# A two-layer encoder in fp32 pairs: the hidden tiles of its feed-forward part in lots of 2, 6, 6, 4 and 4, and weight splits tied to a place in their engines' rows

## The chip, the cores and the metric

The kernel runs on one core of a Trainium2 chip. The metric is device time in microseconds (us), smaller is better. Engines are called by their names in the profile: PE is TensorE (PEld its weight loads), DVE is VectorE, ACT is ScalarE, POOL is GpSimd, SP is SyncE, which here only issues transfers. Each engine works its own row of instructions in order.

## The reference

Two layers over 512 tokens of width 1024, all in fp32. With the mixer A (a window of +-128 tokens) in layer 0 and the mixer B (all tokens) in layer 1:

```
x += rms_norm(w_o [12 token heads | 4 memory heads](rms_norm(x)))
x += rms_norm(SwiGLU(rms_norm(x)))        # silu(h Wg) * (h Wu), then @ Wd
```

The hidden width of SwiGLU is 2816, which is 22 tiles of 128.

## The kernel before, in words

**Pairs.** TensorE works on fp32r. Each fp32 operand is split into a hi part (a copy on ScalarE, L318) and a lo part (a subtraction on VectorE, L322), and each product is three matmuls: hi by hi, hi by lo, lo by hi (L308 to L310 for plain products).

**Lots.** The feed-forward part works the hidden tiles in lots: `LOTS = ((0, 2), (2, 8), (8, 14), (14, 22))`. For each hidden tile from the third on, gate and up come from seven block products (`seven`, L1131 to L1133, 256 columns, 84 matmuls a tile) in the manner of Strassen. When the last block of a tile is done, ScalarE takes Silu (L1184), VectorE multiplies by up (L1185), and `keep_hidden` splits the hidden tile into its pair: hi on ScalarE (L1007), lo on VectorE (L1008). With its first or second half of the lot's tiles, the sums and differences that the seven down products need are formed too (`low`, `high`, L1020 to L1031).

**Down.** The lots in `SEVEN` (the second and third, six tiles each) get their part of the down product as seven block products too (`down` calls `times`, L1257 to L1259, 512 columns): A11, A12, S2, S1, S3, S4, A22 in this order. Each result is added to the layer's output `o` in SBUF (`out_of`, L1267). A11's last steps and A12 follow the last tile's last block at once, so those of the steps that take older tiles stand first (`BY_UNIT`), and the last tile's come at the thirteenth matmul. The weights' block sums are made by transfers that add (`load_block`, the queue of POOL); `pairs` splits them. The last lot's down product is plain (`ffn_out`): for each row block of 128 tokens and each half of 512 columns three matmuls a tile, then `join` adds to `o` (L928), forms the mean square on ScalarE (L346), multiplies by the gain (L932); `post_norm` adds the residual (L814) and, in layer 0, writes the next layer's normed rows `h` (L822), which TensorE turns and VectorE and ScalarE split (`hrows`). In layer 1 the last row block is worked in two quarters (`ending`, L946, L950).

**Spares.** During the down products of layer 0's lots of six, `spare_load` fetches weights wq and wo of layer 1, and `spare_pair` splits them in halves (`c<-raw` on ScalarE, `s<-raw,c` on VectorE) and stores the pairs in DRAM; layer 1 then loads pairs. What is left of these units is split by `ahead` during the last lot's plain down product.

**Order.** TensorE's order is written out by hand. The rows of ScalarE, VectorE, POOL and SP are laid by a scheduler, which goes by its own estimates; `queue` and `issue_after` tie an instruction behind another. The pool of split weights holds four pairs, that of raw weights three.

## Time and profile before

| | |
|---|---|
| median of three runs | 1089.26 us (1089.0 to 1090.06) |
| profiled execution | 1091.68 us, its span 1089.9 us |
| TensorE busy | 1063.6 us (98%), 7364 matmuls |
| VectorE busy | 894.2 us (82%) |
| ScalarE busy | 693.5 us (64%) |
| granted clock of TensorE, mean | 0.994 |

Times in the rows of the trace count from the start of the span. A row of the timeline has the start, the duration, engine, line, operation, output and inputs, and in brackets how long the engine was idle before it and what released it. Rows of windows have the stretch, its length, the busy time of PE, PEld, DVE, ACT and POOL with their counts, then TensorE's granted clock, the share of the transfer engines and GB/s. Matmul durations overlap; what counts is the distance from start to start.

### The profile page before, as it was taken

To read this page: it belongs to the slowest core of one execution; us is meant where nothing else is said; L and a number is where in the kernel's file an instruction comes from. 1 tells how busy PE (TensorE), PEld (TensorE's weight loads), DVE (VectorE), ACT (ScalarE), POOL (GpSimd) and SP (SyncE) were. 2 spreads that over 40 slices of the span, in tenths; PEclk is the share of its full clock that TensorE was granted. 3 is DMA by queue.
4 is the path that set the end of the run, shared out by engine and by line. 5 is a ranking of instruction groups with operands and counts; after the bars stand their busy time and mean duration, and the time that the engine had idled before them with its cause. 6 is when DMAs were issued, how large, how long until landed. Compare 5 with 4: busy or idle time off the path is not lost.

```text
span 1089.9 us, 19990 instructions
## 1 busy us (share of the span) xinstructions
PE 1063.6 (98%) x7364; PEld 973.2 (89%) x7364; DVE 894.2 (82%) x1561; ACT 693.5 (64%) x1429; POOL 255.3 (23%) x405
## 2 busy tenths in 40 slices
PE   9999999999999989999999999999999999999997
PEld 7899887999879979998898888778999899899986
DVE  7889875978899979995887998767979888899954
ACT  7679884766646645663566888766766466556631
POOL 5673331211131100000443553313011111100001
PEclk9999999999999999999999999999999999999999
DMA  9721106456987894329752220136369769833243
GB/s 326 265 67 39 33 20 258 148 134 173 264 272 181 233 273 166 110 67 317 242 193 98 78 78 1 47 119 227 104 149 261 219 162 255 220 113 105 68 162 116
DMA packets 56978, 173.42 MB, mean 159 GB/s; under 512 B 6576, under 2 KB 6960, under 8 KB 56752
## 3 DMA queue, kind: packets, MB, share of 16 engines
q1 hardware_dynamic: 47376, 150.76, 40.4%
q0 software_dynamic: 9216, 20.98, 11.4%
q8 instruction: 58, 0.95, 0.4%
q10 hardware_dynamic: 288, 0.40, 0.1%
q14 instruction: 40, 0.33, 0.1%
HBM read 149.04 MB, written 16.78 MB: 152 GB/s over the span
## 4 chain that ended last, share of the span: by engine, by line
PE 82%; DVE 7%; ACT 4%; DMA 3%; issue 2%; POOL 2%; SPq 0%; DVEq 0%; POOLq 0%; ACTq 0%
PE ps L1131 11%; PE ps L1132 11%; PE ps L1133 11%; PE ps L309 9%; PE ps L308 9%; PE ps L310 9%; PE ps L1259 3%; PE ps L1257 3%; PE ps L1258 3%; PE tp L673 3%; PE o L687 2%; PE o L688 2%; PE s L612 1%; DMA raw<-in_wq_dram 1%; PE s L613 1%
## 5 line engine op out<-in xcount | busy, mean ns | idle before, releaser
L318 ACT ACTIVATE whi<-raw 128x512 fp32r<-128x512 f32 (+3 forms) x180 | 141.2, 804 | 93.6 <-issue 26.0
L322 DVE TENSOR_TENSOR wlo<-raw,whi 128x512 fp32r<-128x512 f32 (+3 forms) x176 | 157.8, 912 | 38.3 <-ACT whi L318 37.8
L1131 PE MATMUL ps<-hrows,whi 128*128 128x256 f32 x640 | 176.3, 275 | 0.1
L1132 PE MATMUL ps<-hrows,wlo 128*128 128x256 f32 x640 | 176.2, 275 | 0.0
L1133 PE MATMUL ps<-hrows,whi 128*128 128x256 f32 x640 | 176.2, 275 | 0.0
L308 PE MATMUL ps<-whi,hrows 128*128 128x256 f32 (+2 forms) x432 | 144.1, 333 | 0.0
L309 PE MATMUL ps<-wlo,hrows 128*128 128x256 f32 (+2 forms) x432 | 138.0, 319 | 1.6 <-DVE wlo L322 1.5
L310 PE MATMUL ps<-whi,hrows 128*128 128x256 f32 (+2 forms) x432 | 138.0, 320 | 0.0
L1132 PE MATMUL ps<-a,wlo 128*128 128x256 f32 x480 | 132.1, 275 | 0.0
L1131 PE MATMUL ps<-a,whi 128*128 128x256 f32 x480 | 132.1, 275 | 0.0
L1133 PE MATMUL ps<-a,whi 128*128 128x256 f32 x480 | 132.1, 275 | 0.0
L1131 PEld LDWEIGHTS ps<-hrows,whi 128*128 128x128 f32 x640 | 120.1, 188 | 0.8 <-ACT p L1137 0.3
L1132 PEld LDWEIGHTS ps<-hrows,wlo 128*128 128x128 f32 x640 | 120.1, 188 | 0.5
L1133 PEld LDWEIGHTS ps<-hrows,whi 128*128 128x128 f32 x640 | 120.1, 188 | 0.0
L663 POOL TENSOR_SCALAR p<-p,rd 128x256 f32<-128x256 f32 (+2 forms) x128 | 78.1, 628 | 102.8 <-DVE rd L660 66.2
L1132 PEld LDWEIGHTS ps<-a,wlo 128*128 128x128 f32 x480 | 90.1, 188 | 0.2
L1131 PEld LDWEIGHTS ps<-a,whi 128*128 128x128 f32 x480 | 90.1, 188 | 0.2
L1133 PEld LDWEIGHTS ps<-a,whi 128*128 128x128 f32 x480 | 90.1, 188 | 0.0
L309 PEld LDWEIGHTS ps<-wlo,hrows 128*128 128x128 f32 x432 | 81.6, 189 | 7.4 <-DVE wlo L322 2.5
L310 PEld LDWEIGHTS ps<-whi,hrows 128*128 128x128 f32 x432 | 81.3, 188 | 5.6 <-DVE hrows L336 0.3
L308 PEld LDWEIGHTS ps<-whi,hrows 128*128 128x128 f32 x432 | 81.4, 188 | 5.0
L318 ACT ACTIVATE whi<-rb 128x1024 fp32r<-128x1024 f32 x56 | 59.6, 1064 | 29.9 <-PE ps L1259 20.7
(231 smaller groups left out, 2854.0 us busy)
## 6 DMA issues: line engine op xcount, KB each, us to landing
raw<-in_wgu_dram SPq DMA_DIRECT2D x48, 512.0 KB, 4.6
rb<-in_wgu_dram SPq DMA_DIRECT2D x40, 512.0 KB, 3.9
raw<-in_wd_dram SPq DMA_DIRECT2D x18, 512.0 KB, 4.3
raw<-in_wq_dram SPq DMA_DIRECT2D x16, 512.0 KB, 5.3
raw<-in_wo_dram SPq DMA_DIRECT2D x16, 512.0 KB, 3.6
rb<-in_ws_dram SPq DMA_DIRECT2D x16, 512.0 KB, 7.6
rs<-in_ws_dram SPq DMA_DIRECT2D x28, 256.0 KB, 6.5
xt<-x SPq DMA_DIRECT2D x12, 512.0 KB, 4.9
```

The costliest lines, as they stand in the source:

```text
L308: mm(out, lh, rh, start=first, stop=False)
L309: mm(out, lh, rl, start=False, stop=False)
L310: mm(out, ll, rh, start=False, stop=last)
L318: a = nc.scalar.activation(hi, src, AF.Copy)
L322: b = nc.vector.tensor_sub(lo, src, hi.bitcast(F32))
L663: self.pooled = nc.gpsimd.tensor_scalar(hd["p"][z][:, :n], hd["p"][z][:, :n], rd[:, z:z + 1], 1.0, op0=OP.mult, op1=OP.mult)
L673: nc.tensor.transpose(tp[:, z], hd["p"][i][:, jj * P:(jj + 1) * P], self.ident)
L1131: mm(out, wh[:, s], rh, start=start and k == 0, stop=False, skip_group_check=True)
L1132: mm(out, wl[:, s], rh, start=False, stop=False, skip_group_check=True)
L1133: mm(out, wh[:, s], rl, start=False, stop=k == 3, skip_group_check=True)
L1257: mm(ps[t], lh, rh, start=fresh and i == 0, stop=False, skip_group_check=True)
L1258: mm(ps[t], lh, rl, start=False, stop=False, skip_group_check=True)
```

## The change

The last lot of eight tiles becomes two lots of four, and the first of these gets its down product as seven block products, with two tiles to a half. `SEVEN` now says how many tiles a half has. The block arrays of the weights become one per lot (`ws1` to `ws3`), a half of two tiles needs no third unit (`rs`), and A11 is cut into 2 + 2 steps where a half of three has 4 + 2 (`fill`). The spare splits: `spare_pair` stands one product later, behind the split of that product's weights, and each of its splits is tied behind the last weight split on ScalarE and on VectorE (`ends["pair"]`). `spare_load` does nothing in the lot of four, so that of two units which `ahead` worked in layer 0 only one is left, and layer 1 splits one wo unit itself.

```
-LOTS = ((0, 2), (2, 8), (8, 14), (14, 22))
-SEVEN, HALF = (1, 2), 3
+LOTS = ((0, 2), (2, 8), (8, 14), (14, 18), (18, 22))
+SEVEN = {1: 3, 2: 3, 3: 2}
...
                 hi, lo = [self.whl.tile([P, 1024], F32R, tag=z, name=f"w{z}", bufs=4) for z in ("hi", "lo")]
-                self.split(hi[:, :n], lo[:, :n], x)
+                ends["pair"] = self.split(hi[:, :n], lo[:, :n], x)
...
-        BY_ROW = [(i, t) for t in range(2) for i in range(HALF)]
-        BY_UNIT = [(0, 0), (1, 0), (0, 1), (1, 1), (2, 0), (2, 1)]
+        def by_row(h):
+            return [(i, t) for t in range(2) for i in range(SEVEN[h["lot"]])]
+
+        def by_unit(h):
+            return [(0, 0), (1, 0), (0, 1), (1, 1), (2, 0), (2, 1)][:2 * SEVEN[h["lot"]]]
+
+        def fill(h, z):
+            n = 2 * SEVEN[h["lot"]] - 2
+            return by_unit(h)[n:] if z else by_unit(h)[:n]
...
-        def spare_load():
-            if self.todo:
+        def spare_load(h):
+            if self.todo and SEVEN[h["lot"]] > 2:
...
                     hi, lo = temp("c"), temp("s")
-                    self.split(hi.bitcast(F32R), lo.bitcast(F32R), x[:, c])
+                    a, b = ends["pair"]
+                    with self.tc.issue_after(a), self.tc.issue_after(b):
+                        ends["pair"] = self.split(hi.bitcast(F32R), lo.bitcast(F32R), x[:, c])
...
             w = pairs(h["t1"])
             y = [self.tagged("pv"), self.tagged("t")]
-            times(y, h, "S1", w, BY_ROW, True)
-            spare_pair()
+            times(y, h, "S1", w, by_row(h), True)
             out_of(y, 1, 1)
             w = pairs(h["t3"])
-            times(x, h, "S3", w, BY_ROW, False)
+            spare_pair()
+            times(x, h, "S3", w, by_row(h), False)
```

Of the instructions, TensorE loses 180 matmuls of 512 columns and 24 of 256 in the plain products and gains 168 of 512 in `times`. In the changed kernel a line behind the first edits has a number up to twelve higher: L1184 to L1186 are L1185 and L1186 there, L1257 to L1259 are L1260 to L1262, L1267 is L1277; the lines of `ffn_out`, `join` and `ending` keep theirs.

Places where instructions move follow. First, ScalarE at the end of a lot of six in layer 0. `c<-raw` is the copy of a spare, `whi` are hi halves of weights, `s<-ps` is the last tile's Silu, L1007 `f<-s` its hi half. Before:

```order
L318 ACTIVATE whi<-rs 128x512
L318 ACTIVATE c<-raw 128x512
L318 ACTIVATE whi<-ru 128x1024
L1184 ACTIVATE s<-ps 128x256
L318 ACTIVATE whi<-rs 128x512
L1007 ACTIVATE f_4231<-s 128x512
L318 ACTIVATE c<-raw 128x512
L318 ACTIVATE whi<-ru 128x1024
```

After:

```order
L318 ACTIVATE whi<-rs 128x512
L318 ACTIVATE whi<-ru 128x1024
L1185 ACTIVATE s<-ps 128x256
L318 ACTIVATE whi<-rs 128x512
L1007 ACTIVATE f_4231<-s 128x512
L318 ACTIVATE whi<-ru 128x1024
L318 ACTIVATE f_4238<-q 128x512
L1007 ACTIVATE f_4243<-k 128x256
L318 ACTIVATE whi<-rs 128x512
L318 ACTIVATE whi<-rb 128x1024
L318 ACTIVATE whi<-rs 128x512
L318 ACTIVATE c<-raw 128x512 x2
```

Both spare copies moved from around the last tile's Silu and hi half to behind them.

Second, VectorE in layer 0's tail: L928, L932, L814 and L822 of the row blocks, the turned rows `hrows`, and the last weight subtractions of the next layer (`wlo<-raw`, 128x768, TensorE's first weights there). Before, from row block 2's L928 to the last of these weights:

```order
L928 TENSOR_TENSOR o<-o,ps 128x512
L322 TENSOR_TENSOR hrows<-tp,hrows 128x4x128 x2
L932 TENSOR_TENSOR o<-o,gain 128x512
L814 SCALAR_TENSOR_TENSOR o<-o,ro,xt 128x512 x2
L322 TENSOR_TENSOR wlo<-raw,whi 128x768
L822 TENSOR_TENSOR h<-o,gain 128x1024
L322 TENSOR_TENSOR wlo<-raw,whi 128x768 x2
L322 TENSOR_TENSOR hrows<-tp,hrows 128x4x128 x2
L928 TENSOR_TENSOR o<-o,ps 128x512
L322 TENSOR_TENSOR wlo<-raw,whi 128x768
```

After, from row block 2's L928 to the last of these weights:

```order
L928 TENSOR_TENSOR o<-o,ps 128x512
L322 TENSOR_TENSOR wlo<-raw,whi 128x768
L322 TENSOR_TENSOR hrows<-tp,hrows 128x4x128
L932 TENSOR_TENSOR o<-o,gain 128x512
L814 SCALAR_TENSOR_TENSOR o<-o,ro,xt 128x512 x2
L322 TENSOR_TENSOR hrows<-tp,hrows 128x4x128
L822 TENSOR_TENSOR h<-o,gain 128x1024
L322 TENSOR_TENSOR wlo<-raw,whi 128x768
```

Of the four weight subtractions one stood ahead of block 2's L822, two behind it and the last behind block 3's L928; now two stand far ahead, among the first halves, one behind block 2's L928 and the last right behind block 2's L822. Ahead of these rows, `h` of block 0 now stands between L928 and L932 of block 1.

Third, VectorE at the end of layer 1. Before:

```order
L814 SCALAR_TENSOR_TENSOR o<-o,ro,xt 128x512 x2
L928 TENSOR_TENSOR o<-o,ps 128x512
L932 TENSOR_TENSOR o<-o,gain 128x512
L814 SCALAR_TENSOR_TENSOR o<-o,ro,xt 128x512 x2
L946 TENSOR_TENSOR o<-o,ps 128x256
L950 TENSOR_TENSOR og<-o,gain 128x256
L946 TENSOR_TENSOR o<-o,ps 128x256
L950 TENSOR_TENSOR og<-o,gain 128x256
```

After:

```order
L814 SCALAR_TENSOR_TENSOR o<-o,ro,xt 128x512 x2
L928 TENSOR_TENSOR o<-o,ps 128x512
L946 TENSOR_TENSOR o<-o,ps 128x256
L950 TENSOR_TENSOR og<-o,gain 128x256
L932 TENSOR_TENSOR o<-o,gain 128x512
L814 SCALAR_TENSOR_TENSOR o<-o,ro,xt 128x512 x2
L946 TENSOR_TENSOR o<-o,ps 128x256
L950 TENSOR_TENSOR og<-o,gain 128x256
```

The first quarter of the last row block moved ahead of row block 2's L932 and L814; the rest of the order stays.

## The prediction

> **What bounds the kernel now.** I read the page first (engines, then the chain), then the waits of TensorE, then windows around those waits beside the same code in the other layer.

> ```profile
> span 1089.9 us, 19990 instructions
> PE 1063.6 (98%) x7364; PEld 973.2 (89%) x7364; DVE 894.2 (82%) x1561; ACT 693.5 (64%) x1429; POOL 255.3 (23%) x405
> PE 82%; DVE 7%; ACT 4%; DMA 3%; issue 2%; POOL 2%; SPq 0%; DVEq 0%; POOLq 0%; ACTq 0%
> ```

> TensorE is busy for 98% of the span and carries 82% of the chain, so time comes from fewer matmuls, from holes in TensorE's row, or from matmuls at a low clock. VectorE at 82% is the next in line: where a stage asks less of TensorE and not less of VectorE, VectorE takes over. The holes are few, and two of them are one place:

> ```profile
> PE ps L1257 <- ACT f L1007: 5.5, 2, 2.9
> PE ps L309 <- DVE wlo L322: 2.0, 3, 0.8
> ```

> These two waits, 5.5 us together, lie in layer 0 at the ends of the two lots of six tiles. The windows hold those ends in layer 0 (first two) and in layer 1 (last two); the column behind POOL is the granted clock.

> ```profile
> 295.00:325.50 30.50, 27.44 (x117) 22.03 (x116) 24.90 (x37) 13.23 (x20) 8.90 (x11) 0.94 0.91 297
> 387.50:417.00 29.50, 26.73 (x110) 21.26 (x110) 25.06 (x38) 14.33 (x21) 2.65 (x3) 0.94 0.85 277
> 851.70:876.60 24.90, 24.90 (x111) 20.25 (x110) 23.69 (x35) 11.50 (x16) 4.44 (x5) 1.00 0.69 188
> 938.00:963.00 25.00, 25.00 (x112) 20.35 (x111) 22.95 (x34) 11.64 (x16) 2.67 (x3) 1.00 0.64 180
> ...
> 299.00:302.40 3.40, 0.77 (x3) 0.33 (x3) 3.40 (x6) 2.29 (x5) 0.86 (x1) 1.00 1.06 352
> 302.40:305.80 3.40, 3.40 (x8) 2.72 (x9) 3.21 (x7) 1.96 (x4) 0.88 (x1) 0.50 1.08 221
> 128.30:131.70 3.40, 1.87 (x14) 1.27 (x13) 2.97 (x11) 3.38 (x11) 0.40 (x1) 1.00 0.00 0
> 131.80:135.20 3.40, 3.40 (x11) 3.11 (x12) 1.88 (x6) 2.47 (x7) 1.72 (x3) 0.50 0.51 154
> ```

> About 111 matmuls go without a hole in 24.9 us in layer 1 and need 30.5 and 29.5 in layer 0. TensorE's idle time there is 30.50 - 27.44 = 3.06 and 29.50 - 26.73 = 2.77. The rest is the clock: a stretch of 3.4 us with a hole in it (0.77 and 1.87 us busy) is followed by 3.4 us at 0.50, which costs half of it, 1.7. Lost in layer 0: 3.06 + 2.77 + 2 x 1.7 = 9.2 us. Its cause stands on ScalarE's row:

> ```profile
> 297.33 0.63 ACT L318 ACTIVATE c<-raw 128x512 fp32r<-128x512 f32 x1 [3.59 <-DMA raw<-in_wq_dram]
> ...
> 298.82 0.36 ACT L1184 ACTIVATE s<-ps 128x256 f32<-128x256 f32 x1
> ...
> 300.08 0.68 DVE L1185 TENSOR_TENSOR s<-s,c 128x512 f32<-128x512 f32 x1
> ...
> 300.80 0.63 ACT L1007 ACTIVATE f<-s 128x512 fp32r<-128x512 f32 x1 [1.11 <-DVE s L1185]
> ...
> 301.49 0.50 PE L1257 MATMUL ps<-whi,f 128*128 128x512 f32 x1 [2.91 <-ACT f L1007]
> ```

> The copy of a spare weight (`c<-raw`) waits 3.59 us for its transfer in ScalarE's row, ahead of the last tile's Silu (L1184), on which L1185, the hidden tile's hi half (L1007) and TensorE hang.

> **The change, part by part.** First the undisturbed end of a lot, in layer 1, which gives two prices:

> ```profile
> 851.62 0.39 PE L1257 MATMUL ps<-whi,f 128*128 128x512 f32 x1
> ...
> 852.70 0.69 DVE L1185 TENSOR_TENSOR s<-s,c 128x512 f32<-128x512 f32 x1
> ...
> 854.24 0.69 DVE L1008 SCALAR_TENSOR_TENSOR f<-s,f 128x512 fp32r<-128x512 f32 x1
> ...
> 854.37 0.39 PE L1257 MATMUL ps<-whi,f 128*128 128x512 f32 x1
> ```

> Twelve matmuls of 512 columns lie between the two L1257 rows: 2.75/12 = 0.229 us each, at issue. And the last tile's pair is done 854.24 + 0.69 - 851.62 = 3.3 us after A12 begins; those twelve matmuls, on older tiles, cover it.

> (1) *Matmuls.* The lot 14-18 takes 7 x 4 x 3 = 84 matmuls in each layer where the plain product took 4 x 8 x 3 = 96. 24 fewer over both: -5.5 us, all on the path.

> (2) *Spares behind an order edge.* In the new row of ScalarE the two spare copies stand behind the last tile's Silu and L1007, so that the end of a lot looks like layer 1's. Gain 9.2; the bounds are 8.2 (VectorE, 24.90 of 30.50 busy there, still carries the spares' subtractions later in the down product, and one slip of half a microsecond at each end is possible) and 9.5. I take -9.2. The extra VectorE work of the change (28 additions L1267 and 12 wide subtractions among it) lies beside TensorE elsewhere, except in the tails below.

> (3) *The end of the new lot, once in each layer.* Here A12 has two tiles, and its second step needs the lot's last tile: cover is 3 matmuls, 0.69 us, where lots of six have twelve. By layer 1's row the lo half comes 3.3 us after A12 begins and is wanted at 5 x 0.229 = 1.15: 2.2 us late. One more weight copy (1.06 us on ScalarE) stands ahead of Silu in the new row and a wide subtraction ahead of L1186; I take 2.5, with 2.2 and 3.5 (the whole copy in the way) as ends. Two layers: +5.0. A hole of that length in one window brings the slow window too: by the row behind 128.30:131.70, where 1.53 us of idle time sufficed, 1.7 us each; not certain, as the hole can straddle two windows, so 1.3 each: +2.6.

> (4) *The tail of layer 0.* The plain product of the last lot now has 4 tiles, 96 matmuls or 22.0 us less TensorE work between the last block of L1133 and the next layer's first weights, while the four row blocks' norms on VectorE stay.

> ```profile
> 495.91 0.39 PE L308 MATMUL ps<-whi,f 128*128 128x512 f32 x1
> ...
> 521.32 0.69 DVE L928 TENSOR_TENSOR o<-o,ps 128x512 f32<-128x512 f32 x1 [0.32 <-PE ps L310]
> 522.86 0.69 DVE L932 TENSOR_TENSOR o<-o,gain 128x512 f32<-128x512 f32 x1 [0.85 <-ACT junk L346]
> 524.27 1.42 DVE L814 SCALAR_TENSOR_TENSOR o<-o,ro,xt 128x512 f32<-128x512 f32 x2 [0.72 <-POOL ro L357]
> 525.72 1.22 DVE L822 TENSOR_TENSOR h<-o,gain 128x1024 f32<-128x1024 f32 x1
> 526.86 0.68 DVE L928 TENSOR_TENSOR o<-o,ps 128x512 f32<-128x512 f32 x1
> ...
> 541.87 0.68 DVE L928 TENSOR_TENSOR o<-o,ps 128x512 f32<-128x512 f32 x1
> 542.47 0.95 DVE L322 TENSOR_TENSOR wlo<-raw,whi 128x768 fp32r<-128x768 f32 x1
> ...
> 543.48 0.45 PE L309 MATMUL ps<-wlo,hrows 128*128 128x384 f32 x1 [0.79 <-DVE wlo L322]
> ```

> L928 to the end of the L814 pair is 4.40 us a row block (521.32 to 525.72), of which 2.95 pass before L814 can start; L822 takes 1.14, L928 0.60 to the next start, a 768-wide weight subtraction about 0.9, one `hrows` 0.6. The last of four weight subtractions (542.47) is what TensorE waits for at 543.48. In the new row of VectorE it stands behind three row blocks: block 0, 4.40; L928 of block 1, h of block 0, then L814 of block 1 ends at 8.80; hrows, h, hrows, L928 of block 2 to 11.74, L814 of block 2 ends at 11.14 + 4.40 = 15.54; hrows and h to 17.28, the subtraction to 18.2. Block 0 starts, by its 25.4 us after 495.91, less 60 matmuls (13.7), at 11.7; so the weight is there at 11.7 + 18.2 = 29.9 us. TensorE, with 22.0 us less to do, would be there at 543.48 - 495.91 - 22.0 = 25.6: 4.3 us late. On top, the last hidden tile comes later, because the split of a spare wo unit and of the weights between stand close together and wait for each other's buffers until a store to DRAM has landed:

> ```profile
> pair<-whi SPq DMA_DIRECT2D x2, 512.0 KB, 5.0
> pair<-wlo SPq DMA_DIRECT2D x2, 512.0 KB, 6.5
> ```

> With 5.0 and 6.5 us from issue, I count the last tile's lo half at 6.2 us after 495.91's counterpart where TensorE wants it at 3.9: +2.3. I take 6.6, with a slow window behind it 7.9. Ends: 0, if enough of the row is slack that the trace doesn't show, and 12, if the norm's gain vector or the wo store's slots come later still.

> (5) *The tail of layer 1.* The same, without new weights:

> ```profile
> 1041.87 0.39 PE L308 MATMUL ps<-whi,f 128*128 128x512 f32 x1
> ...
> 1066.58 0.69 DVE L928 TENSOR_TENSOR o<-o,ps 128x512 f32<-128x512 f32 x1 [2.25 <-PE ps L310]
> ...
> 1083.20 0.42 DVE L946 TENSOR_TENSOR o<-o,ps 128x256 f32<-128x256 f32 x1 [0.61 <-PE ps L310]
> ...
> 1085.89 0.74 DVE L814 SCALAR_TENSOR_TENSOR o<-og,ro,xt 128x512 f32<-128x512 f32 x1
> ```

> Before, TensorE needs 24 x 0.229 = 5.5 us for a row block, more than VectorE's 4.40; now 2.75. In the new row the blocks 0, 1 and 2 are worked through before the last L946. Block 0 starts 24.7 - 13.7 = 11.0 us after the counterpart of 1041.87, three chains end at 24.2, and from the last L946 to the end of the span are 1089.9 - 1083.2 = 6.7: 30.9. Without a loss it would be 1089.9 - 1041.87 - 22.0 = 26.0. +4.8 (4.0 to 5.5).

> (6) One wo unit of layer 1 is no longer split in layer 0 and is split in the mixer instead: some 2.3 us on ScalarE and VectorE beside TensorE's row; +0.5, between 0 and 1.

> Sum: -5.5 - 9.2 + 5.0 + 2.6 + 7.9 + 4.8 + 0.5 = +6.1 us against the profiled execution of 1091.68 (span 1089.9), so 1097.8; the median of the runs is 1089.26, 2.4 below, so 1095.4.

> [...]

> **The rivals.**

> *Slower, by VectorE's row and the clock*, my forecast: 1092 to 1099.

> *VectorE's row is no bound in the tails* (faster). If row blocks overlap, so that a block costs VectorE what it is busy (0.69 + 0.69 + 1.42 = 2.8 us) and not 4.40, it keeps up with 2.75 of TensorE: the terms (4) and (5) go, +6.1 - 12.7 = -6.6, 1082.7. The order of the rows speaks against it in layer 1, where each L814 pair comes before the next block's L928; in layer 0 the blocks do overlap in part. It decides from where three blocks take less than about 9 us.

> *No clock loss and half the tail* (same): holes split over windows, without the late last tile: -5.5 - 9.2 + 5.0 + 4.3 + 4.8 + 0.5 = -0.1, 1089.2. For it speaks that each of these terms has a free phase.

> [...]

> *A transfer comes late*: the pair stores, or the block sum that a weight copy ahead of L1007 waits for; 5 us more at a tail or a lot's end: 1100.

> *The edge doesn't keep the spares out of the way*: the 9.2 stay, 1104.6. The new row of ScalarE speaks against it.

> **How the numbers follow.** The forecast has 0.47, a late transfer 0.13, the spares' failure 0.02, the gate rule 0.08 (half of it slower), no clock loss with half the tail 0.13, VectorE no bound 0.17. What can be told from no change here is 0.2%, 2.2 us: below 1087.1 is faster, above 1091.4 slower. Slower: 0.47 + 0.13 + 0.02 + 0.04 = 0.66; same: 0.13 + 0.04 = 0.17; faster 0.17. The range leaves a tenth out at each end: 1084 (two thirds of the faster case lie below or about it) to 1100.5. The forecast's own range is 1092 to 1099.

> **What would show it.** Right: no wait of L1260 for L1007 above 0.5 us in layer 0's lots of six; a wait of about 1.9 us and one of 0.5 to 1 at the second step of A12 in the lot 14-18, in both layers, followed by 3.4 us at 0.50; TensorE waiting 5 us or more for the last weight's lo half in layer 0's tail; in layer 1 TensorE's last matmul some 11 us before the end of the span, not 6.7. Wrong: tails whose L928 rows wait for TensorE as before, or a wait at a place that I hold covered, the other steps of the new lot's seven products above all.

## The result, and the profile after

The changed kernel takes 1103.36 us (median of 4 runs, 1101.35 to 1107.84), the kernel before 1089.66 (4 runs): 1.3% slower, ratio 1.0133 with a 95% interval of 1.0113 to 1.0154. The forecast, 1095.4 with a range to 1100.5, had the sign and 6.1 us of the 13.7. Of the later executions two ran at a much lower clock, one of the kernel before (1757.19 us, mean granted clock 0.557) and one of e12 (1168.29 us, 0.849), and the ratios leave both out. In the changed kernel the last tile's Silu is L1185, the multiply by up L1186, and the matmuls of `seven` are L1132 to L1134. Rows of the page of the profiled execution (1102.34 us) and of TensorE's waits:

```profile
span 1100.6 us, 20105 instructions
PE 1060.4 (96%) x7328; PEld 967.9 (88%) x7328; DVE 920.8 (84%) x1616; ACT 703.2 (64%) x1448; POOL 263.2 (24%) x421
...
PE tp L380 <- DVE h L822: 4.3, 2, 3.0
PE ps L309 <- DVE wlo L322: 4.0, 2, 3.2
...
PE ps L1260 <- ACT f L1007: 3.5, 2, 1.7
PE ps L1261 <- DVE wlo L322: 2.9, 2, 2.6
```

TensorE is busy 3.2 us less and the span is 10.7 us longer: all of the loss is waiting. 4.8 us of it lie behind TensorE's last matmul, and the waits that are new in TensorE's row name VectorE for the most part. Read off TensorE's row, stage by stage (us, in the two profiled executions; T runs from the last matmul of a lot's last tile to the first of the next tile, with 108 matmuls between them for a lot of six and 72 for the new lot):

| stage | before | after | difference |
|---|---|---|---|
| start to the first tile of layer 0's seven block products | 234.1 | 231.7 | -2.4 |
| T, layer 0, first and second lot of six | 29.9, 29.6 | 29.2, 25.5 | -4.8 |
| first tile behind the second lot, layer 0 | 9.6 | 10.7 | +1.1 |
| T of the new lot, each layer (16.6 without a hole) | | 19.1 | +2.5, +2.5 |
| matmuls saved, 24 x 0.229 | | | -5.5 |
| last block of seven in layer 0 to the first of layer 1 | 294.0 | 284.3 | +12.3 beside 22.0 less work |
| last block of seven in layer 1 to the end | 47.9 | 30.7 | +4.8 beside 22.0 less work |

The sum is +10.5, beside 10.7 by the spans. The first row is the same code in both: the kernel before came out of its hole at 130 us later (at 131.70 against 130.73) and had a slow window behind it, a stretch of 3.4 us at half the clock, at 131.8; the changed one had none. Without this row the two executions are 13 apart, like the medians.

The windows around the lots' ends, as before the prediction (the first two of six tiles in layer 0, then the new lot in layer 0 and 1):

```profile
293.20:322.50 29.30, 26.68 (x112) 21.30 (x111) 24.59 (x37) 12.27 (x19) 5.97 (x10) 0.94 0.88 282
383.80:409.40 25.60, 25.31 (x112) 20.20 (x111) 23.26 (x35) 12.18 (x18) 2.54 (x3) 1.00 0.79 246
451.50:470.70 19.20, 17.12 (x76) 13.57 (x75) 18.95 (x29) 8.10 (x10) 0.88 (x1) 1.00 0.43 114
1009.70:1028.90 19.20, 17.12 (x76) 13.58 (x75) 18.70 (x29) 8.10 (x10) 0.88 (x1) 1.00 0.47 124
```

The second lot of six is mended nearly as forecast, 25.6 for 29.5 with 0.3 idle. The first is not: 2.6 us idle again and a clock of 0.94. Its timeline shows that the wait has only changed its place:

```profile
307.79 0.36 SPq L1102 DMA_DIRECT2D rb<-in_wgu_dram  x1
...
313.77 0.69 DVE L1110 TENSOR_TENSOR ru<-raw,rb 128x512 f32<-128x512 f32 x1 [3.11 <-DMA rb<-in_wgu_dram]
...
315.71 1.22 DVE L322 TENSOR_TENSOR wlo<-rb,whi 128x1024 fp32r<-128x1024 f32 x1
...
316.98 0.79 PE L1261 MATMUL ps<-wlo,f 128*128 128x512 f32 x1 [2.62 <-DVE wlo L322]
```

L1110, the next lot's first addition, waits 3.11 us for a gate/up weight that SP issued at 307.79. Behind it in VectorE's row stands the lo half of the last block product's weights, on which TensorE waits. The spares no longer hold ScalarE; something else now holds VectorE.

The new lot's end, and layer 0's tail (rows of several engines, in order of time):

```profile
453.43 0.63 ACT L1007 ACTIVATE f<-s 128x512 fp32r<-128x512 f32 x1 [0.39 <-DVE s L1186]
454.11 0.50 PE L1260 MATMUL ps<-whi,f 128*128 128x512 f32 x1 [1.74 <-ACT f L1007]
...
511.46 0.39 PE L308 MATMUL ps<-whi,f 128*128 128x512 f32 x1
...
515.29 0.43 SPq L364 DMA_DIRECT2D gain<-in_g_ffn_post_dram  x1
...
522.87 1.90 DVE L932 TENSOR_TENSOR o<-o,gain 128x512 f32<-128x512 f32 x3 [1.68 <-DMA gain<-in_g_ffn_post_dram]
...
526.83 0.68 DVE L928 TENSOR_TENSOR o<-o,ps 128x512 f32<-128x512 f32 x1
...
532.98 1.09 PE L380 MATMUL tp<-cst,h 128*128 128x128 f32 x8 [2.99 <-DVE h L822]
538.10 1.17 PE L380 MATMUL tp<-cst,h 128*128 128x128 f32 x8 [1.30 <-DVE h L822]
...
545.02 0.95 DVE L322 TENSOR_TENSOR wlo<-raw,whi 128x768 fp32r<-128x768 f32 x1
...
546.02 0.69 PE L309 MATMUL ps<-wlo,hrows 128*128 128x384 f32 x1 [3.19 <-DVE wlo L322]
```

L308 at 511.46 is the first matmul of the plain product, and L928 at 526.83 is the join that completes row block 0. TensorE waits in the tail for each stage of VectorE's row in turn: for `h` of the first two row blocks and for the last weight's lo half.

### The profile page after: what moved, and what is told of

Read it like the earlier page. It is cut to its first block, busy times and chain, and to the rows that moved or that the text cites. A ratio compares the mean times of both kernels' runs of the same rounds, so it can differ in the third digit from the quotient of the medians.

```text
span 1100.6 us, 20105 instructions
## 1 busy us (share of the span) xinstructions
PE 1060.4 (96%) x7328; PEld 967.9 (88%) x7328; DVE 920.8 (84%) x1616; ACT 703.2 (64%) x1448; POOL 263.2 (24%) x421
## 5 line engine op out<-in xcount | busy, mean ns | idle before, releaser
L318 ACT ACTIVATE whi<-raw 128x512 fp32r<-128x512 f32 (+3 forms) x175 | 134.9, 791 | 76.4 <-issue 28.3
L1132 PE MATMUL ps<-hrows,whi 128*128 128x256 f32 x640 | 176.3, 276 | 0.7 <-ACT p L1138 0.7
L1133 PE MATMUL ps<-hrows,wlo 128*128 128x256 f32 x640 | 176.3, 275 | 0.0
L1134 PE MATMUL ps<-hrows,whi 128*128 128x256 f32 x640 | 176.2, 275 | 0.0
L322 DVE TENSOR_TENSOR wlo<-raw,whi 128x512 fp32r<-128x512 f32 (+3 forms) x171 | 150.8, 896 | 22.0 <-ACT whi L318 21.5
L308 PE MATMUL ps<-whi,hrows 128*128 128x256 f32 (+2 forms) x432 | 144.6, 335 | 0.0
L309 PE MATMUL ps<-wlo,hrows 128*128 128x256 f32 (+2 forms) x432 | 138.7, 321 | 4.0 <-DVE wlo L322 4.0
L310 PE MATMUL ps<-whi,hrows 128*128 128x256 f32 (+2 forms) x432 | 138.5, 321 | 0.0
L1133 PE MATMUL ps<-a,wlo 128*128 128x256 f32 x480 | 132.3, 276 | 0.0
L1132 PE MATMUL ps<-a,whi 128*128 128x256 f32 x480 | 132.1, 275 | 0.0
L1134 PE MATMUL ps<-a,whi 128*128 128x256 f32 x480 | 132.1, 275 | 0.0
L1132 PEld LDWEIGHTS ps<-hrows,whi 128*128 128x128 f32 x640 | 120.2, 188 | 1.5 <-ACT p L1138 0.9
L1133 PEld LDWEIGHTS ps<-hrows,wlo 128*128 128x128 f32 x640 | 120.1, 188 | 0.7
L1134 PEld LDWEIGHTS ps<-hrows,whi 128*128 128x128 f32 x640 | 120.2, 188 | 0.0
L318 ACT ACTIVATE whi<-rb 128x1024 fp32r<-128x1024 f32 x64 | 68.1, 1064 | 38.9 <-PE ps L1262 20.4
L1261 PE MATMUL ps<-wlo,f 128*128 128x512 f32 x224 | 88.8, 397 | 2.9 <-DVE wlo L322 2.9
L1260 PE MATMUL ps<-whi,f 128*128 128x512 f32 x224 | 88.0, 393 | 3.5 <-ACT f L1007 3.5
L309 PEld LDWEIGHTS ps<-wlo,hrows 128*128 128x128 f32 x432 | 82.1, 190 | 9.9 <-DVE wlo L322 5.0
L1133 PEld LDWEIGHTS ps<-a,wlo 128*128 128x128 f32 x480 | 90.1, 188 | 0.5 <-DVE wlo L322 0.2
L1132 PEld LDWEIGHTS ps<-a,whi 128*128 128x128 f32 x480 | 90.1, 188 | 0.3
L1134 PEld LDWEIGHTS ps<-a,whi 128*128 128x128 f32 x480 | 90.1, 188 | 0.0
## 6 DMA issues: line engine op xcount, KB each, us to landing
raw<-in_wgu_dram SPq DMA_DIRECT2D x48, 512.0 KB, 5.5
rb<-in_wgu_dram SPq DMA_DIRECT2D x40, 512.0 KB, 4.3
rb<-in_ws_dram SPq DMA_DIRECT2D x24, 512.0 KB, 7.1
raw<-in_wq_dram SPq DMA_DIRECT2D x16, 512.0 KB, 4.9
raw<-in_wo_dram SPq DMA_DIRECT2D x16, 512.0 KB, 3.6
ru<-in_ws_dram SPq DMA_DIRECT2D x12, 512.0 KB, 6.2
xt<-x SPq DMA_DIRECT2D x12, 512.0 KB, 4.6
```

Source lines behind the costliest of these rows:

```text
L308: mm(out, lh, rh, start=first, stop=False)
L309: mm(out, lh, rl, start=False, stop=False)
L310: mm(out, ll, rh, start=False, stop=last)
L318: a = nc.scalar.activation(hi, src, AF.Copy)
L322: b = nc.vector.tensor_sub(lo, src, hi.bitcast(F32))
L1132: mm(out, wh[:, s], rh, start=start and k == 0, stop=False, skip_group_check=True)
```

## The experiments

Each time is a median, beside the kernel before on the same chip (1088.3 to 1088.8). "Changed" is the changed kernel, 1103.36; it was not run again beside the experiments, so what is said against it rests on the ratios, or on stages of the profiles, of which there is one for each kernel.

**The parts alone.** e1, the edge without the new lots:

```
-LOTS = ((0, 2), (2, 8), (8, 14), (14, 18), (18, 22))
-SEVEN = {1: 3, 2: 3, 3: 2}
+LOTS = ((0, 2), (2, 8), (8, 14), (14, 22))
+SEVEN = {1: 3, 2: 3}
```

> Only the spare splits are moved and tied; the lots stay 2, 6, 6 and 8. Forecast's step (2): 9.2 us faster than before, some 1080.5. What the changed kernel's trace shows (first lot of six still 29.3 us long with a hole of 2.62, second 25.6 instead of 29.7): 4.5 to 5 us faster, about 1085, with the same hole in the first lot of six, since TensorE waits there for a lo half behind a late gate/up load on VectorE. Rival: the edge gives nothing, the lot's end just shifts: 1089.

1087.17, ratio 0.9979 (0.9964 to 0.9993): 1.7 us faster by the medians. The hole is there without the new lots:

```profile
PE ps L1261 <- DVE wlo L322: 2.7, 2, 2.4
```

The T stages are 29.2 and 25.6, as in the changed kernel, and the first tile behind the second lot is 1.1 longer. So the edge's worth is 3.6 us at these places in the profile and not 9.2. It is less in the medians; in this profile layer 0's tail is 2.9 us longer than before (296.9 for 294.0), with one slow window in it, and e5 below shows a wait there.

e2, the new lots without the edge:

```
-                    a, b = ends["pair"]
-                    with self.tc.issue_after(a), self.tc.issue_after(b):
-                        ends["pair"] = self.split(hi.bitcast(F32R), lo.bitcast(F32R), x[:, c])
+                    self.split(hi.bitcast(F32R), lo.bitcast(F32R), x[:, c])
```

and `spare_pair` one product earlier, as before.

> Only the lots are changed (2, 6, 6, 4, 4 with the seven block products for 14-18); the spare splits stand where they stood before, without the edge. Theory (the two parts add up): before plus 18 us, about 1107. Rival, the edge itself harms the new lot and the tail: below 1100.

1108.55, ratio 1.0184 (1.0169 to 1.0199). The loss is that of the lots; the edge doesn't harm. The lots cost 1.8% without it and 1.3% with it, while the edge alone gains 0.2%, so the two parts do not simply add up.

e3 and e4, the lot of eight cut in one layer alone (with the edge; e3's lines, e4 has `l == 0`):

```
+        LOTS = ((0, 2), (2, 8), (8, 14)) + (((14, 18), (18, 22)) if l == 1 else ((14, 22),))
+        SEVEN = {1: 3, 2: 3, 3: 2} if l == 1 else {1: 3, 2: 3}
```

> With the edge; the lot of eight is cut in layer 1 alone. Theory: e1 plus 2.5 for the new lot's end, plus 4.8 for the tail of layer 1, less 2.7 of matmuls: e1 + 4.6. Without a bound by VectorE in the tail (rival): e1 - 0.2.

1093.41, ratio 1.0042 (1.0028 to 1.0057): e1 + 6.2; by the spans (1091.3 and 1086.5) + 4.8.

> With the edge; the lot of eight is cut in layer 0 alone. Theory from the changed kernel's trace: e1 plus 2.5 (end of the new lot), plus 1.2 (its first tile), plus some 12 for the tail, less 2.7: e1 + 13. The forecast's sizes gave e1 + 8.5 with a clock loss at the lot's end.

1099.43, ratio 1.0103 (1.0079 to 1.0128): e1 + 12.3. Both cuts cost, layer 0's twice as much; 12.3 and 6.2 make 18.5, where the changed kernel is 16.2 above e1 by the medians.

**The first lot's hole.** e5 is e1 with the next lot's first additions behind the last weight's lo half, in layer 0:

```
+            tie = self.tc.issue_after(ends["pair"][1]) if l == 0 and f in [x[0] for x in LOTS[2:]] else nullcontext()
-            with self.tc.issue_after(forms.last[1] if f == 3 else self.flo) if f > 2 else nullcontext():
+            with tie, self.tc.issue_after(forms.last[1] if f == 3 else self.flo) if f > 2 else nullcontext():
```

> e1 with the next lot's first additions (L1110 to L1112, which wait for a gate/up load) tied in layer 0 behind the lo half of the last block product's weights, so that they no longer stand ahead of it on VectorE. Theory (the 2.4 us hole left in the first lot of six is this wait): the hole goes and the slow clock behind it, e1 - 4, about 1083. Rival (the weights' lo half is late in any case, or the next tile's first products wait instead for L1112): a hole of 2 us or more remains, 1087.

1085.57, ratio 0.9980 (0.9969 to 0.9992). Windows of the two lots' ends, and TensorE's wait:

```profile
293.20:318.20 25.00, 25.00 (x112) 20.30 (x110) 21.46 (x32) 12.18 (x19) 7.25 (x10) 1.00 0.91 294
384.60:409.60 25.00, 25.00 (x120) 20.77 (x119) 23.90 (x37) 12.43 (x18) 1.78 (x2) 1.00 0.88 281
...
PE ps L1133 <- ACT p L1139: 1.9, 1, 1.9
```

Both ends are now as in layer 1, 9.5 us less than before for both. But TensorE waits 1.9 us in the next tile's first products, and that tile takes 12.5 us where one without a wait takes 9.6, so the rival is right in part. Layer 0's tail is 1.3 us longer than before, too (295.3 for 294.0), since a first weight of the next layer lands late:

```profile
533.82 0.84 ACT L318 ACTIVATE whi<-raw 128x768 fp32r<-128x768 f32 x1 [2.78 <-DMA raw<-in_wkv_dram]
...
534.72 0.45 PE L308 MATMUL ps<-whi,hrows 128*128 128x384 f32 x1 [1.22 <-ACT whi L318]
```

The same stage takes 296.6 to 297.0 us in e1, e3, e8 and e9, the other kernels with the edge and no cut in layer 0 (with a slow window in it in all but e3). The prediction has no term for this, and why the weight is late was not tried. What is left is 2.8 by the medians, beside 1.7 for e1; their intervals overlap.

e9 is e5 with the rotary table loaded during the second lot of six:

```
...
-            if l == 0 and "rope" not in turn:
+            if l == 0 and h["lot"] == 2 and "rope" not in turn:
...
```

> e5 with the two loads of the rotary table moved from the first lot of six to the second, so that SP's row brings the next lot's gate/up load about 1 us earlier. Theory (the hole of 1.9 us that e5 has left in the first tile after that lot is this load's lateness): that hole shrinks to about 1 us or goes, 1 to 2 us faster than e5, 1084. Rival: the load is late for the transfers' share and not for its place, no change; or the hole appears behind the second lot.

1087.73, ratio 0.9987 (0.9976 to 0.9997): no gain on e5 (0.9980). The first of these windows is the first lot's end; the second reaches from the second lot's end, which has no hole, into the tile behind it. The idle time is now there, and the wait at L1133 keeps its size:

```profile
294.40:319.40 25.00, 25.00 (x113) 20.40 (x112) 24.04 (x36) 12.17 (x18) 2.38 (x3) 1.00 0.92 284
386.00:411.00 25.00, 23.19 (x112) 19.06 (x110) 20.85 (x31) 9.52 (x14) 6.75 (x9) 1.00 0.89 276
...
PE ps L1133 <- ACT p L1139: 1.9, 1, 1.9
```

That tile takes 14.9 us for 9.6, with a slow window in it; the tile behind the first lot takes 9.8. The hole goes where the table's loads go. They make the difference between layer 0's two lots; by which of their ways (SP's row, POOL's, the transfers' share) was not tried apart.

**Layer 0's tail.** e6, the changed kernel with the gain vector on POOL's queue:

```
-        g = self.gain(gpost, "gpost")
+        g = self.npool.tile([P, D], F32, tag="gpost", name="gain", bufs=1)
+        nc.gpsimd.dma_start(g, _rows(gpost, D))
```

> The changed kernel, with the norm's gain vector of the last lot's ending fetched on POOL's queue and not behind SP's others. Theory (the tail of layer 0 begins late since L932 waits for that load, 1.68 us, and all of VectorE's row behind it): the wait goes, the holes ahead of L380 and L309 shrink by 1.7 together or each, 2 to 4 us faster than the changed kernel, 1100. Rival (the tail is bound by the row blocks' chain alone): the wait goes, the hole ahead of L309 stays at 3 us, no gain.

1098.06 (2 runs, 1096.21 and 1099.91), ratio 1.0093 (1.0062 to 1.0125). TensorE's waits:

```profile
PE ps L309 <- DVE wlo L322: 4.1, 2, 3.2
...
PE tp L380 <- DVE h L822: 2.7, 2, 1.4
```

The tail is 279.9 for 284.3. The first L380 hole is 1.4 for 3.0, about the gain vector's 1.68; the hole ahead of L309 keeps its 3.2. From the first plain matmul to the last weight's lo half it is 32.9 us for 34.5. The other 3 us or so are two slow windows that this execution doesn't have. What the load costs differs between executions: in e10, which leaves this place as it is, L932 did not wait for it, and the same stretch is 34.0.

e7, the changed kernel without `ahead` in the tail:

```
                 self.down_prod(ps[t], get, fs, u, t, wu)
-            self.ahead()
```

> The changed kernel without `ahead` in the tail: the wo unit that was split and stored there is split in layer 1. Theory (ScalarE waits 4.86 us for that pair's store to DRAM ahead of the last tile's Silu, and SP's queue behind it brings the gain late): the holes at L1007 and L1008 (0.83 and 0.61) go, the tail's others shrink by 1 to 2, layer 1 loses 0.5 at most: 1100. Rival: other waits take its place, 1103.

1103.71 (2 runs), ratio 1.0145 (1.0117 to 1.0174): no gain, as the rival had it. The waits for L1007 and L1008 in the tail (0.83 and 0.61) are gone, and those at L380 and L309 behind them are 4.0 and 3.5, where the changed kernel has 3.0, 1.3 and 3.2:

```profile
PE ps L309 <- DVE wlo L322: 4.3, 2, 3.5
PE tp L380 <- DVE h L822: 4.0, 1, 4.0
```

The last weight's lo half is ready 33.9 us after the first plain matmul, for 34.5, so 0.6 of the 1.4 us is kept there. In this execution a slow window in layer 0's new lot (T 20.7 for 19.1) costs more than that. So the pair's store, to which the prediction gave 2.3 us, delays a tile that is hardly the bound; as L932 waits 2.72 us for the gain vector here, some cost of the store may be hidden behind that wait.

**Layer 1's tail.** e8 is e3 with L928 of a row block ahead of L814 of the block before:

```
             join(ps, t, 1)
+            if rs is None:
+                if t:
+                    with self.tc.issue_after(self.joined):
+                        late[t - 1]()
+                late[t] = lambda t=t: self.post_norm(...)
+                continue
...
```

> e3 (the lot of eight cut in layer 1 alone) with the rows of VectorE in layer 1's tail in another order: L928 of the next row block stands ahead of L814 of the block before. Theory (the tail is bound by the chain of 4.40 us for each row block in VectorE's row, of which 1.6 is waiting): the time from the last L1134 to the end falls from 30.9 to some 26.5, e3 - 4.4, about 1089. Rival (VectorE's busy time is the bound): 30 and no gain.

1092.32, ratio 1.0034 (1.0019 to 1.0049), e3 - 1.1; the tail is 28.1 for 30.1. VectorE's row:

```profile
1075.97 0.69 DVE L928 TENSOR_TENSOR o<-o,ps 128x512 f32<-128x512 f32 x1 [0.49 <-PE ps L310]
1076.57 1.41 DVE L814 SCALAR_TENSOR_TENSOR o<-o,ro,xt 128x512 f32<-128x512 f32 x2
...
1078.69 0.69 DVE L928 TENSOR_TENSOR o<-o,ps 128x512 f32<-128x512 f32 x1
...
1086.04 0.75 DVE L814 SCALAR_TENSOR_TENSOR o<-o,ro,xt 128x512 f32<-128x512 f32 x1 [1.79 <-DMA xt<-x]
```

A row block now takes 2.72 (1075.97 to 1078.69), TensorE's pace, and not 4.3: the bound was the chain with its waiting, not VectorE's busy time. The tail falls by 2.0 and not by 4.4. The residual rows, which now load late (1.79 above), are 0.6 of what is missing, by e11, where four buffers hold them and the tail is 27.5; the rest stays open. By the medians the gain is not clear of noise: the intervals of e3 and e8 overlap.

**The new lot's end.** e10, the changed kernel with another order of A12's steps:

```
-            times(z, h, "A12", w, by_unit(h), True)
+            times(z, h, "A12", w, by_unit(h) if SEVEN[h["lot"]] > 2 else [(0, 0), (0, 1), (1, 0), (1, 1)], True)
```

> The changed kernel with A12's steps for two tiles in the order (0,0), (0,1), (1,0), (1,1): six matmuls ahead of the last tile's and not three. Theory (the hole at the new lot's end is missing cover): 1.74 us less 3 x 0.229 = 1.05 us in each layer, and the second hole (0.34) goes as well or stays; 1.4 us or 2 over both. Rival (something else ends late there): the hole stays at 1.74.

1099.43 (2 runs, 1098.63 and 1100.23), ratio 1.0098 (1.0078 to 1.0119).

```profile
PE ps L1260 <- ACT f L1007: 2.1, 2, 1.0
```

The hole is 1.04 for 1.74 in each layer: 0.70 less, the three matmuls (0.69) that now lie ahead of it. So the hole is missing cover; T of the new lot is 18.6 for 19.1. The rest of the difference in the medians is not this place's.

**All remedies.** e11 is the changed kernel with e5's tie, e6, e10 and e8 (four buffers for the residual rows of layer 1's tail):

```
...
-        xt = self.npool.tile([P, D], F32, tag="x", name="xt", bufs=2)
+        xt = self.npool.tile([P, D], F32, tag="x", name="xt", bufs=4 if gn is None else 2)
...
```

> The changed kernel with all remedies at once: the tie of e5, the gain vector on POOL's queue, A12's order of e10, and layer 1's tail as in e8 with four buffers for the residual rows. Theory (the cut of the lot of eight costs by these waits, and saves 5.5): changed kernel less 4 (lot's end), 4 (gain), 1.5 (A12), 4 (tail of layer 1), 1090, still above e5 by about the row blocks' chain in layer 0's tail, 5. Rival (these waits are only symptoms, others follow): above 1095; the cut pays after all: below 1085.

1093.57, ratio 1.0048 (1.0031 to 1.0065), between the theory and its rivals. T of both lots of six is 24.9 as in layer 1, that of the new lot 18.6, and layer 1's tail 27.5 for 30.7; layer 0's tail is 280.7 for 284.3, and the hole ahead of L309 is still 3.2.

e12 is e11 with the next layer's first weights split ahead of row block 2's norm:

```
...
                 self.wkv = [self.unit(self.a["wkv"][1, u]) for u in range(4)]
+                with self.tc.issue_after(self.last_lo):
+                    late[t - 1] = self.post_norm(t - 1, ...)
...
```

> e11 with the last of the next layer's first weights split ahead of row block 2's L814 and L822 in layer 0's tail, and not behind them. Theory (TensorE waits there for its place in VectorE's row, behind the row blocks' chain): the 3.2 us hole at L309 falls below 1 us, 2 to 3 us faster than e11, about 1091, unless the later h of row block 2 gives a hole at L380. Rival (the weight itself, or its hi half, comes late): the hole stays.

1092.03, ratio 1.0029 (1.0019 to 1.0040). The last weight's lo half now stands ahead of L814 (L815 here):

```profile
537.73 0.95 DVE L322 TENSOR_TENSOR wlo<-raw,whi 128x768 fp32r<-128x768 f32 x1
538.60 1.41 DVE L815 SCALAR_TENSOR_TENSOR o<-o,ro,xt 128x512 f32<-128x512 f32 x2
```

The 3.2 us hole ahead of L309 is gone, and a smaller one (0.87) has come at L308. Layer 0's tail is not shorter for it in this profile, 281.1 with a slow window in it, and the intervals of e11 and e12 overlap. By the ratios the cut, mended at five places, gets 11 of its 14 us back and is still slower than before, and 0.5% slower than e5, which has the tie and no cut and is the fastest of all.

## Why the prediction was right or wrong, point by point

- **(1) Matmuls, -5.5**: right, and TensorE's busy time fell by 3.2 with the slow windows in it.
- **(2) The edge, -9.2**: the step that failed is "the end of a lot looks like layer 1's". Measured: -4.8 at the two ends and +1.1 behind them, -3.7 (e1: -3.6). The row of ScalarE was read rightly, and no L1260 of a lot of six waits for L1007 any more. VectorE's row was not followed as far: L1110, behind a late transfer, stood there ahead of the last weights' lo half. In layer 1 the same order does no harm (L1110 at 873.09 waits for nothing, and TensorE has no hole in 857.40:882.40); spare pairs and the rotary table load in layer 0 alone, and in e9 the hole moved with the table's loads. e5 shows that 9.5 us can be had at the ends, that 2.9 come back one tile later and 1.3 in the tail.
- **(3) The new lot's end, +2.5 each**: right to a tenth (19.1 for 16.6), with its cause (e10). The clock's +2.6 did not come in this execution: the grid of slow windows (last section) split the 1.74 us hole in layer 0 into 0.61 and 1.13, and in layer 1, where one stretch holds it whole, no slow window followed; in e2 the loss came, where the same stages took 20.5 and 20.7.
- **(4) Layer 0's tail, +7.9 and (6) +0.5**: mis-sized, 12.3. The chain in VectorE's row was right: from block 0's L928 to the end of the last weight's subtraction it takes 19.1 us (526.83 to 545.97), where 18.2 was taken. It begins too late: block 0's L928 stands 15.4 us after the first plain matmul (511.46), and the prediction has 11.7 and 2.3 for the late last tile, 14.0. So the weight is ready after 34.5 us and not 32.2. The late start was put on the pair's store; without that store the weight is 0.6 earlier (e7), with the gain vector on another queue 1.6 (e6), and that load the prediction had only in its upper bound. TensorE's waiting was not foreseen in its place: 3.2 us for the weight, since it had already waited 4.3 for `h`. Two slow windows, up to 3.4 us, stood in for one of 1.3. No run shows (6) by itself.
- **(5) Layer 1's tail, +4.8**: right to a tenth, and so are its parts. Rows of it:

```profile
1080.80 0.69 DVE L928 TENSOR_TENSOR o<-o,ps 128x512 f32<-128x512 f32 x1 [0.49 <-PE ps L310]
...
1085.08 0.68 DVE L928 TENSOR_TENSOR o<-o,ps 128x512 f32<-128x512 f32 x1
...
1089.35 0.68 DVE L928 TENSOR_TENSOR o<-o,ps 128x512 f32<-128x512 f32 x1
...
1096.30 0.74 DVE L814 SCALAR_TENSOR_TENSOR o<-og,ro,xt 128x512 f32<-128x512 f32 x1
```

  Block 0's L928 stands 11.1 us after the first plain matmul (taken: 11.0), row blocks follow each other by 4.28 and 4.27 (4.40), and TensorE's last matmul is 11.5 us before the end (some 11).

Against the forecast of +6.1, then: 5.5 from (2), 3.9 from (4) and (6), less 2.6 from the clock in (3): +12.9, and the execution before was slow by 2.4 in its first stage. Behind the miss in (2), and behind part of that in (4), stands a transfer that was late ahead of a wait in VectorE's row. The rival "a transfer comes late" (0.13) had this in kind, but it named the pair stores and a block sum, and the late ones were a gate/up weight and the gain vector. The rival without a bound in VectorE's row is out, with 12.3 and 4.8 lost in the tails. The 0.08 that the chances give a gate rule has no run behind it: the stretch 541.73:545.14, with 1.10 us of work in it, was followed by half the clock.

## What to carry to other kernels

When work is taken from the bounding engine in a tail, price the tail by the next engine's row: the chain of a row block with its waits (4.3 us here), not its busy time (2.8), and see whether the rows can be interleaved (2.7). An instruction that waits for a transfer is moved out of the way only if what stands behind it in every engine's row is looked at too; here the same microseconds showed at L1257, then L1261, then L1133. A lot's end needs matmuls on older data to cover the last tile's way through ScalarE and VectorE, 3.3 us here; a lot of four leaves three matmuls of cover where one of six leaves twelve, and the way is no shorter (3.6 us there, from L1260 at 451.51 to the end of L1008 at 455.13).

## What the runs showed of the hardware that was not expected

All slow windows of an execution start at whole multiples of 3.413 us from each other, in the twelve of fourteen profiles that have more than one (50, 77 and 280 of them behind the first in the kernel before). Whether a hole brought one differed with where it fell: the 1.37 us hole at 130 us, the same code in every kernel, was followed by a slow window in 4 of 14 profiles (in the kernel before, where the stretch 128.34:131.75 was idle for 1.53, and not in the changed one, where 128.72:132.13 was idle for 1.37), the 1.74 us hole of the new lot in 3 of 11, and holes of 2.2 to 4.0 in layer 0 in 15 of 20.

```profile
541.73:545.14 3.41, 1.10 (x7) 0.79 (x5) 3.19 (x5) 1.45 (x4) 1.10 (x3) 1.00 0.66 259
545.00:551.80 6.80, 5.78 (x21) 5.68 (x22) 4.04 (x7) 1.73 (x4) 2.54 (x4) 0.51 0.46 153
...
1009.36:1012.77 3.41, 1.67 (x10) 1.04 (x8) 3.41 (x6) 2.23 (x4) 0.72 (x1) 1.00 0.27 107
```
